# A decoder layer in split float32: the low part of half of w_down's weights made by ACT and a GpSimd DMA

## The chip, the cores and the metric

One core of a Trainium2 chip runs the kernel. The metric is the device time of one execution in microseconds (us); lower is better.

## The reference

One layer of a hybrid decoder on 256 tokens of 2048 features, in float32. Two token mixers run side by side, their gated sum goes through `w_out`, and then come an MLP and a gated embedding:

```python
h = rmsnorm(x, g_mix);  proj = h @ w_in
ya = dilated_mixture(qa, ka, va);  yb = stick_breaking(qb, kb, vb)
x = x + (sigmoid(ga) * (ya @ w_branch_a) + sigmoid(gb) * (yb @ w_branch_b)) @ w_out
x = x + square(relu(rmsnorm(x, g_mlp) @ w_up)) @ w_down
x = x + (p @ w_ple_proj) * sigmoid(rmsnorm(x, g_ple) @ w_ple_gate)
```

`w_up` is 2048 x 8192 and `w_down` 8192 x 2048.

## The kernel before

Every product is made from float32r parts. A number is written as a high part (its rounding to float32r) and a low part (the number minus the high part), both float32r. A product of weight and activation is the sum of three products of parts: high with high, high with low, low with high. In `group_t` the high part of a weight tile of 128 x 128 meets both parts of the activation at once, 512 columns (line 135), and the low part of the weight meets the high part of the activation, 256 columns (line 136). These two matmuls are called a pair here. A group gives two output tiles of 128 features and goes over 16 k tiles, so it has 32 pairs.

Weights come in loads of 1 MB (8 k tiles of 256 columns) into a tile `raw`, by DMAs that SP issues (line 88). `split_weights` cuts a load into two halves of 1024 columns each. For each half, ACT copies `raw` into `wh`, which rounds it (line 79), and VectorE (DVE) writes `wl = raw - wh` (line 80). The tags `raw`, `wh` and `wl` have three buffers each, in the pool `wts`; a buffer is used again when its last reader is done: PE for `wh` and `wl`, ACT and DVE for `raw`.

The MLP goes by quarters of its 8192 hidden features. A quarter is 8 groups of `w_up` (its result, squared and split, is `u`), then 8 groups of `w_down`, each over the quarter's 16 k tiles: two loads a group, `c` = 0 and 1. `residual` adds a group's result to `x` (ACT copies one half out of PSUM, line 447, and DVE adds twice, lines 448 and 449). In the last quarter it also splits the next product's input `h3` (lines 82 and 83) and adds up squares on GpSimd (Pool): `xq` and `acc` (lines 457 and 458).

Large activations lie in blocks of 8 KB per partition, of which the pool `blk` has 15: `x` takes 2, `h`, `m`, `h2`, `u` and `h3` 4 each, `ya`, `yb` and the gate `ga` 2 each, and `qT`, `kT`, `va`, `qS`, `kS`, `vb` one each. Small tiles of 256 columns share the tag `w1` with 8 buffers.

The order of the instructions on each engine is made by the tile framework's planner from the program's order, the buffers that are free and its own costs; each engine then runs its queue in order and waits on semaphores. `later` and `advance` put the attention heads and the embedding's products between the groups by estimated times.

Of the kernel before, what the change touches and what calls it, by code (L numbers as in the profile page):

```python
# [10 lines left out]
F32R = mybir.dt.float32r  # L11
# [5 lines left out]
P = 128  # L17
# [42 lines left out]
def layer_kernel(ctx: ExitStack, tc: tile.TileContext, xt, pt, gains, qkg, cst,  # L60
                 wa, wb, wba, wbb, wo, wup, wdn, wpg, wpp, out):
    nc = tc.nc
    const = ctx.enter_context(tc.tile_pool(name="const", bufs=1))
    blk = ctx.enter_context(tc.tile_pool(name="blk", bufs=15))
    wts = ctx.enter_context(tc.tile_pool(name="wts", bufs=3))
# [10 lines left out]
    def split(hi, lo, src, scale=None):  # L76
        """src (times a per-partition scale) as the exact sum of two float32r parts."""
        if scale is None:
            nc.scalar.activation(hi, src, AF.Copy)  # L79
            nc.vector.tensor_tensor(lo, src, hi.bitcast(F32), op=ALU.subtract)  # L80
        else:
            nc.scalar.activation(hi, src, AF.Copy, scale=scale)
            nc.vector.scalar_tensor_tensor(lo, src, scale, hi.bitcast(F32),  # L83
                                           op0=ALU.mult, op1=ALU.subtract)
# [5 lines left out]

    def split_weights(raw, nk, cols, step=None):
        """The two parts of each k tile of a loaded weight."""
        step = step or 1024 // cols
        parts = []
        for k0 in range(0, nk, step):
            n = min(step, nk - k0)
            wh = wts.tile([P, n, cols], F32R, tag="wh", name="wh")
            wl = wts.tile([P, n, cols], F32R, tag="wl", name="wl")
            split(wh, wl, raw[:, k0:k0 + n, :])
            parts += [(wh[:, i, :], wl[:, i, :]) for i in range(n)]  # L100
        return parts

    def weights(src, nk, cols):
        return split_weights(load(src, nk, cols), nk, cols)

# [3 lines left out]
    def later(us, fn, *args):  # L109
        """Emit fn once the products emitted from here on take this long on the tensor engine."""  # L110
        pending.append((clock[0] + us, len(pending), fn, args))
# [14 lines left out]
    def group_t(chunks, rhs, tag="mm"):  # L126
        """Two feature-major output tiles [P, 512]: columns 0:256 and 256:512 add up to the result.
        A chunk is a source in memory or the parts of its k tiles."""
        ps = [bank(tag) for _ in range(2)]
        last, kt = len(rhs) - 1, 0  # L130
        for src in chunks:
            for wh, wl in src if isinstance(src, list) else weights(src, 8, 256):
                for j in range(2):
                    c = slice(j * P, (j + 1) * P)
                    nc.tensor.matmul(ps[j], wh[:, c], flat(rhs[kt]), start=kt == 0, stop=False)  # L135
                    nc.tensor.matmul(ps[j][:, :T], wl[:, c], rhs[kt][:, 0, :], start=False,  # L136
                                     stop=kt == last)
                kt += 1
                advance(0.65)
        return ps  # L140

    def group_m(chunks, lhs, load=lambda src: weights(src, 4, 512)):
        """Token-major output [2][P tokens, 512 columns]."""
        ps = [bank("mm") for _ in range(2)]
        last, kt = len(lhs) - 1, 0
        for src in chunks:
            for wh, wl in load(src):
                for tt in range(2):
                    t = slice(tt * P, (tt + 1) * P)
                    nc.tensor.matmul(ps[tt], lhs[kt][:, 0, t], wh, start=kt == 0, stop=False)  # L150
                    nc.tensor.matmul(ps[tt], lhs[kt][:, 0, t], wl, start=False, stop=False)  # L151
                    nc.tensor.matmul(ps[tt], lhs[kt][:, 1, t], wh, start=False, stop=kt == last)  # L152
                kt += 1
                advance(1.3)
        return ps

    def halves(ps):
        """Sum of the two halves of a feature-major result, in SBUF."""
        t = work.tile([P, T], F32, tag="w1", name="ev", bufs=W1)
        s = work.tile([P, T], F32, tag="w1", name="es", bufs=W1)  # L160
        nc.scalar.activation(t, ps[:, T:], AF.Copy)  # L161
        nc.vector.tensor_tensor(s, ps[:, :T], t, op=ALU.add)  # L162
        return s

    def rsqrt(y, v, n):
        """y = v ** -0.5, [P, n]; v is kept."""
        s = work.tile([P, n], F32, tag=f"rs{n}", name="rs_s", bufs=1)
        nc.scalar.activation(s, v, AF.Sqrt)
        nc.vector.reciprocal(y, s)
        nc.vector.tensor_tensor(s, y, y, op=ALU.mult)  # L170
        nc.vector.tensor_tensor(s, s, v, op=ALU.mult)
        nc.vector.tensor_scalar(s, s, -0.5, 1.5, op0=ALU.mult, op1=ALU.add)
        nc.vector.tensor_tensor(y, y, s, op=ALU.mult)

    def norm_rows(sq, tag):
        """Reciprocal root mean square of each token, on all partitions: [P, T]."""
        ps = bank("at")
        nc.tensor.matmul(ps[:, :T], ones, sq, start=True, stop=True)
        v = work.tile([P, T], F32, tag="w1", name="nv", bufs=W1)
        nc.vector.tensor_scalar(v, ps[:, :T], 1.0 / D, EPS, op0=ALU.mult, op1=ALU.add)  # L180
        rb = work.tile([P, T], F32, tag="rb", name=tag, bufs=1)
        rsqrt(rb, v, T)
        return rb

# [1 line left out]
    x = [block([P, 8, T], F32, f"x{i}") for i in range(2)]  # L186
# [21 lines left out]

# [1 line left out]
    h = new_acts("h")  # L210
# [4 lines left out]
    def first_weights(c):  # L215
        """x and the first weights in turn, in the order in which the products take them."""
        k = 4 * c
        if c == 0:
            raw = wts.tile([P, 4, 512], F32, tag="raw", name="raw")
            for a, b in ((0, 1), (1, 2), (2, 4)):  # L220
                load_x(a, b)
                nc.sync.dma_start(raw[:, a:b, :].rearrange("p k c -> p (k c)"),
                                  wa[0, 0, :, a * 512:b * 512])
        else:
            load_x(k, k + 4)
            raw = load(wa[0, c], 4, 512)
        for i in range(k, k + 4):
            split(h[i][:, 0, :], h[i][:, 1, :], xs(i), gn[:, 0, i:i + 1])
        if c == 3:
            nc.sync.dma_start(cs, cst)  # L230
            nc.sync.dma_start(gq, bass.AP(tensor=qkg.tensor, offset=qkg.offset,
                                          ap=[[0, P], [DH, 2], [1, DH]]))
        return split_weights(raw, 4, 512, 1 if c == 0 else 2)
# [22 lines left out]

# [1 line left out]
    qT = block([P, NH, T], F32, "qT")  # L258
# [56 lines left out]
    def attend(y, hd, at, v):  # L315
        """y[hd] = (at^T @ v)^T, at [keys, 0:256] for the first key tile, [keys, 256:384] for the second."""
        o = bank("at")
# [70 lines left out]

# [1 line left out]
    ya = new_acts("ya", NH)  # L390
# [11 lines left out]

# [1 line left out]
    yb = new_acts("yb", NH)  # L404
# [21 lines left out]

# [1 line left out]
    m = new_acts("m")  # L428
# [15 lines left out]
    def residual(k, ps, h, gain, acc):  # L444
        """x += result; the next product's input, and the sum of squares."""
        t = work.tile([P, T], F32, tag="w1", name="ev", bufs=W1)
# [21 lines left out]

# [1 line left out]
    em, eparts = [], []  # L470
# [23 lines left out]

# [1 line left out]
    for q in range(4):  # L496
# [14 lines left out]
        for g in range(8):  # L511
            ps = group_t([wdn[g, 2 * q + c] for c in range(2)], u)
            for j in range(2):
                residual(2 * g + j, ps[j], h3 if q == 3 else None, 2, acc)
    later(8, lambda: rbs.append(norm_rows(acc, "rb2")))

# [1 line left out]
    def gate_out(k, s):  # L518
        """out = x + embedding * sigmoid(gate / rms), the gate from memory or accumulators."""
        g = work.tile([P, T], F32, tag="w1", name="g", bufs=W1)  # L520
# [22 lines left out]
def tiles_t(w, nk=8):  # L543
    """[K, N] -> [N / 256, K / (128 nk), 128, nk 256]: what one load takes is contiguous."""
    k, n = w.shape
# [4 lines left out]
def tiles_m(w):  # L550
    """[K, N] -> [N / 512, K / 512, 128, 4 512]."""
    k, n = w.shape
# [4 lines left out]
def columns(a):  # L557
    """[T, K] -> [128, K / 128, T]."""
    t, k = a.shape
# [40 lines left out]
```

## Time and profile before

| what | value |
|---|---|
| median of 3 runs | 1495.04 us |
| lowest and highest run | 1492.69 and 1505.25 us |
| span of the profiled execution | 1494.2 us |
| PE, DVE, ACT, Pool busy in it | 1480.9, 1007.3, 783.1, 133.7 us |
| DMA queue of SP | 275.76 MB, 52.3% of 16 engines |

The profile is one execution. Its span is the time from its first to its last instruction, and it has no other time of its own. PE is the matmul engine, PEld its weight loads, which overlap with matmuls. A busy PE is not PE at its peak, because matmuls are pipelined and their ends are modelled.

### The profile page before, as it was taken

What the parts mean: (1) busy time and instruction counts of PE and PEld (TensorE: products, weight loads), DVE (VectorE), ACT (ScalarE), POOL (GpSimd) and SP (SyncE); (2) the same over time, 40 slices, a digit from 0 to 9 for tenths busy, and PEclk for the clock granted to TensorE, in tenths of its full rate; (3) what the DMA queues carried; (4) which work ended last, traced back from release to release, by engine and by line L of the source; (5) the groups of instructions that cost most, each with busy time, mean ns of one, the idle gap of its engine ahead of it and who ended that gap; (6) DMA issues with size and microseconds to landing.
All of it is one profiled execution on the core that took longest, in us unless ns stands there. A gap on an engine that the chain in (4) does not pass through costs nothing.

```text
span 1494.2 us, 20920 instructions
## 1 busy us (share of the span) xinstructions
PE 1480.9 (99%) x8252; PEld 1285.3 (86%) x8252; DVE 1007.3 (67%) x1463; ACT 783.1 (52%) x1130; POOL 133.7 (9%) x137
## 2 busy tenths in 40 slices
PE   8999999999999999999999999999999999999998
PEld 6788888888888888888888888888888888888887
DVE  7875666466676667767766567656676567777776
ACT  6454554489845555555544445444454445555553
POOL 3432000000000000441000000000000000024200
PEclk9999999999999999999999999999999999999999
DMA  7455444544455555555555555555555555555563
GB/s 297 150 193 190 173 157 163 191 170 168 153 193 197 174 193 188 179 197 175 193 197 187 184 194 197 184 185 196 194 182 189 197 179 187 198 177 189 189 211 109
DMA packets 41281, 277.10 MB, mean 185 GB/s; under 512 B 4704, under 2 KB 7136, under 8 KB 8288
## 3 DMA queue, kind: packets, MB, share of 16 engines
q1 hardware_dynamic: 41040, 275.76, 52.3%
q8 instruction: 64, 1.05, 0.3%
q14 instruction: 33, 0.27, 0.1%
q10 hardware_dynamic: 144, 0.02, 0.0%
HBM read 273.67 MB, written 2.10 MB: 185 GB/s over the span
## 4 chain that ended last, share of the span: by engine, by line
PE 96%; DVE 2%; DMA 0%; ACT 0%; POOL 0%; issue 0%; SPq 0%; ACTq 0%; DVEq 0%; POOLq 0%
PE ps_mm L135 55%; PE ps_mm L136 28%; PE ps_mm L151 3%; PE ps_mm L152 3%; PE ps_mm L150 3%; DVE wl L80 1%; PE ps_at L135 0%; DMA x<-in_xt 0%; PE ps_at L319 0%; DVE h L83 0%; PE ps_mm L537 0%; PE ps_mm L539 0%; PE ps_mm L538 0%; PE ps_at L136 0%; PE ps_at L320 0%
## 5 line engine op out<-in xcount | busy, mean ns | idle before, releaser
L80 DVE TENSOR_TENSOR wl<-raw,wh 128x1024 fp32r<-128x1024 f32 (+1 forms) x518 | 636.2, 1229 | 361.6 <-ACT wh L79 355.2
L79 ACT ACTIVATE wh<-raw 128x1024 fp32r<-128x1024 f32 (+1 forms) x518 | 546.1, 1055 | 461.4 <-PE ps_mm L135 369.8
L135 PE MATMUL ps_mm<-h,wh 128*128 128x512 f32 x2016 | 712.3, 397 | 0.0
L136 PE MATMUL ps_mm<-h,wl 128*128 128x256 f32 x2016 | 564.7, 280 | 0.0
L135 PEld LDWEIGHTS ps_mm<-h,wh 128*128 128x128 f32 x2016 | 377.8, 187 | 87.0 <-ACT wh L79 0.3
L136 PEld LDWEIGHTS ps_mm<-h,wl 128*128 128x128 f32 x2016 | 380.8, 189 | 0.5
L135 PE MATMUL ps_mm<-u,wh 128*128 128x512 f32 x1024 | 356.9, 393 | 0.0
L136 PE MATMUL ps_mm<-u,wl 128*128 128x256 f32 x1024 | 286.9, 280 | 0.0
L135 PEld LDWEIGHTS ps_mm<-u,wh 128*128 128x128 f32 x1024 | 191.7, 187 | 43.6
L136 PEld LDWEIGHTS ps_mm<-u,wl 128*128 128x128 f32 x1024 | 193.5, 189 | 0.0
L161 ACT ACTIVATE ev<-ps_mm 128x256 f32<-128x256 f32 x158 | 59.7, 378 | 91.9 <-PE ps_mm L136 91.9
L150 PE MATMUL ps_mm<-wh,h 128*128 128x512 f32 x256 | 101.7, 400 | 2.6 <-ACT wh L79 2.6
L151 PE MATMUL ps_mm<-wl,h 128*128 128x512 f32 x256 | 101.5, 397 | 2.0 <-DVE wl L80 1.9
L454 POOL TENSOR_TENSOR acc<-x 128x256 f32<-128x256 f32 x2 | 3.3, 1653 | 1112.9 <-DVE x L449 1112.9
L152 PE MATMUL ps_mm<-wh,h 128*128 128x512 f32 x256 | 101.4, 396 | 0.0
L162 DVE TENSOR_TENSOR es<-ps_mm,ev 128x256 f32<-128x256 f32 x158 | 66.4, 421 | 44.2 <-ACT ev L161 44.0
L135 PE MATMUL ps_mm<-m,wh 128*128 128x512 f32 x256 | 90.5, 399 | 0.0
L136 PE MATMUL ps_mm<-m,wl 128*128 128x256 f32 x256 | 71.9, 281 | 0.0
L150 PEld LDWEIGHTS ps_mm<-wh,h 128*128 128x128 f32 x256 | 49.0, 192 | 14.8 <-ACT wh L79 4.9
L447 ACT ACTIVATE ev<-ps_mm 128x256 f32<-128x256 f32 x80 | 30.3, 379 | 59.0 <-PE ps_mm L136 59.0
L151 PEld LDWEIGHTS ps_mm<-wl,h 128*128 128x128 f32 x256 | 49.0, 191 | 13.8 <-DVE wl L80 3.8
L135 PEld LDWEIGHTS ps_mm<-m,wh 128*128 128x128 f32 x256 | 48.1, 188 | 12.1
(159 smaller groups left out, 1181.9 us busy)
## 6 DMA issues: line engine op xcount, KB each, us to landing
raw<-in_wup SPq DMA_DIRECT2D x64, 1024.0 KB, 4.7
raw<-in_wdn SPq DMA_DIRECT2D x64, 1024.0 KB, 4.8
raw<-in_wb SPq DMA_DIRECT2D x48, 1024.0 KB, 4.8
raw<-in_wa SPq DMA_DIRECT2D x31, 1024.0 KB, 4.8
raw<-in_wo SPq DMA_DIRECT2D x16, 1024.0 KB, 4.7
raw<-in_wpg SPq DMA_DIRECT2D x16, 1024.0 KB, 4.8
raw<-in_wba SPq DMA_DIRECT2D x8, 1024.0 KB, 4.7
raw<-in_wbb SPq DMA_DIRECT2D x8, 1024.0 KB, 4.7
```

What stands on the lines that cost most here:

```text
L79: nc.scalar.activation(hi, src, AF.Copy)
L80: nc.vector.tensor_tensor(lo, src, hi.bitcast(F32), op=ALU.subtract)
L135: nc.tensor.matmul(ps[j], wh[:, c], flat(rhs[kt]), start=kt == 0, stop=False)
L136: nc.tensor.matmul(ps[j][:, :T], wl[:, c], rhs[kt][:, 0, :], start=False, stop=kt == last)
L150: nc.tensor.matmul(ps[tt], lhs[kt][:, 0, t], wh, start=kt == 0, stop=False)
L151: nc.tensor.matmul(ps[tt], lhs[kt][:, 0, t], wl, start=False, stop=False)
L152: nc.tensor.matmul(ps[tt], lhs[kt][:, 1, t], wh, start=False, stop=kt == last)
L161: nc.scalar.activation(t, ps[:, T:], AF.Copy)
L162: nc.vector.tensor_tensor(s, ps[:, :T], t, op=ALU.add)
L447: nc.scalar.activation(t, ps[:, T:], AF.Copy)
L454: nc.gpsimd.tensor_tensor(acc, xs(k), xs(k), op=ALU.mult)
```

## The change

In `w_down`, the load `c` = 0 of each group gets its low part in another way. ACT writes the negated, rounded weight into `wl` (a copy with scale -1), then `wh` as before, and a DMA issued from GpSimd adds `raw` to `wl` in place. DVE's subtraction falls away there. The load `c` = 1 is split as before, and so are all other weights. The tags `wh` and `wl` get a fourth buffer, in the whole kernel, and the pool of blocks goes from 15 to 14. A source given to `group_t` may now be a function, called when its turn comes.

```diff
-    blk = ctx.enter_context(tc.tile_pool(name="blk", bufs=15))
+    blk = ctx.enter_context(tc.tile_pool(name="blk", bufs=14))
...
-    def split_weights(raw, nk, cols, step=None):
+    def split_weights(raw, nk, cols, step=None, by_dma=False):
...
-            wh = wts.tile([P, n, cols], F32R, tag="wh", name="wh")
-            wl = wts.tile([P, n, cols], F32R, tag="wl", name="wl")
-            split(wh, wl, raw[:, k0:k0 + n, :])
+            wh = wts.tile([P, n, cols], F32R, tag="wh", name="wh", bufs=4)
+            wl = wts.tile([P, n, cols], F32R, tag="wl", name="wl", bufs=4)
+            if by_dma:
+                src = raw[:, k0:k0 + n, :]
+                nc.scalar.activation(wl, src, AF.Copy, scale=-1.0)
+                nc.scalar.activation(wh, src, AF.Copy)
+                nc.gpsimd.dma_start(wl.rearrange("p k c -> p (k c)"),
+                                    src.rearrange("p k c -> p (k c)"), accum_op=ALU.add)
+            else:
+                split(wh, wl, raw[:, k0:k0 + n, :])
...
-    def weights(src, nk, cols):
-        return split_weights(load(src, nk, cols), nk, cols)
+    def weights(src, nk, cols, by_dma=False):
+        return split_weights(load(src, nk, cols), nk, cols, by_dma=by_dma)
...
-            for wh, wl in src if isinstance(src, list) else weights(src, 8, 256):
+            parts = src if isinstance(src, list) else src() if callable(src) else weights(src, 8, 256)
+            for wh, wl in parts:
...
-            ps = group_t([wdn[g, 2 * q + c] for c in range(2)], u)
+            ps = group_t([lambda c=c: weights(wdn[g, 2 * q + c], 8, 256, by_dma=c == 0)
+                          for c in range(2)], u)
```

## Rows read from the trace of the kernel before

**Rows 1.** The page's busy table and the head of its chain.
```profile
PE 1480.9 (99%) x8252; PEld 1285.3 (86%) x8252; DVE 1007.3 (67%) x1463; ACT 783.1 (52%) x1130; POOL 133.7 (9%) x137
...
PE 96%; DVE 2%; DMA 0%; ACT 0%; POOL 0%; issue 0%; SPq 0%; ACTq 0%; DVEq 0%; POOLq 0%
```

**Rows 2.** Timeline of PE in two w_down stages: start us, us, engine, line, op, tiles.
```profile
784.74 0.39 PE L135 MATMUL ps_mm<-u,wh 128*128 128x512 f32 x1
...
814.90 0.39 PE L135 MATMUL ps_mm<-u,wh 128*128 128x512 f32 x1
...
1375.72 0.40 PE L135 MATMUL ps_mm<-u,wh 128*128 128x512 f32 x1
...
1383.84 0.40 PE L135 MATMUL ps_mm<-u,wh 128*128 128x512 f32 x1
```

**Rows 3.** Stretches: us; busy PE, PEld, DVE, ACT, POOL; granted clock; DMA share; GB/s.
```profile
20.00:30.00 10.00, 8.54 (x36) 6.39 (x36) 10.00 (x11) 6.10 (x11) 5.74 (x6) 1.00 0.67 247
10.00:20.00 10.00, 8.38 (x34) 6.11 (x33) 8.35 (x11) 9.85 (x19) 6.66 (x8) 1.00 1.01 422
763.50:852.00 88.50, 88.50 (x513) 78.05 (x512) 53.41 (x68) 39.12 (x50) 0.00 (x0) 1.00 0.54 191
1310.00:1399.00 89.00, 89.00 (x506) 77.13 (x505) 63.63 (x81) 44.95 (x63) 33.36 (x27) 1.00 0.53 188
```

**Rows 4.** Waits between 662 and 1400 us: total us, times, longest.
```profile
ACT wh L79 <- PE ps_mm L135: 257.4, 189, 1.8
DVE wl L80 <- ACT wh L79: 192.7, 158, 1.8
...
PEld ps_mm L135 <- ACT wh L79: 0.3, 1, 0.3
```

**Rows 5.** Groups of instructions in 763.5 to 852 us: busy us, mean ns.
```profile
L80 DVE TENSOR_TENSOR wl<-raw,wh 128x1024 fp32r<-128x1024 f32 x32 | 39.2, 1225 | 29.6 <-ACT wh L79 29.2
L79 ACT ACTIVATE wh<-raw 128x1024 fp32r<-128x1024 f32 x32 | 33.9, 1060 | 37.2 <-PE ps_mm L135 37.2
...
L447 ACT ACTIVATE ev<-ps_mm 128x256 f32<-128x256 f32 x14 | 5.3, 381 | 10.3 <-PE ps_mm L136 10.3
```

**Rows 6.** Timeline of ACT in the first w_down.
```profile
799.73 1.06 ACT L79 ACTIVATE wh<-raw 128x1024 fp32r<-128x1024 f32 x1 [1.40 <-PE ps_mm L135]
```

**Rows 7.** The tile `raw`: issues by SP, ns min/median/max, first and last start.
```profile
L88 SPq DMA_DIRECT2D raw<-in_wdn x64: 327/328/328, 746.9 to 1376.4; - x64
```

**Rows 8.** Timeline of a group's end in the last w_down, without PE.
```profile
1342.70 0.38 ACT L447 ACTIVATE ev<-ps_mm 128x256 f32<-128x256 f32 x1 [1.46 <-PE ps_mm L136]
...
1344.14 1.62 POOL L457 TENSOR_TENSOR xq<-x 128x256 f32<-128x256 f32 x1 [5.95 <-ACT wh L79]
...
1345.84 0.81 POOL L458 TENSOR_TENSOR acc<-acc,xq 128x256 f32<-128x256 f32 x1
...
1347.01 1.61 POOL L457 TENSOR_TENSOR xq<-x 128x256 f32<-128x256 f32 x1 [0.36 <-DVE x L449]
...
1354.01 0.38 ACT L447 ACTIVATE ev<-ps_mm 128x256 f32<-128x256 f32 x1 [1.47 <-PE ps_mm L136]
```

**Rows 9.** DMA issues: count, KB each, median us from issue to landing.
```profile
raw<-in_wdn SPq DMA_DIRECT2D x64, 1024.0 KB, 4.8
...
x<-in_xt SPq DMA_DIRECT2D x3, 512.0 KB, 10.0
...
raw<-in_wa SPq DMA_DIRECT2D x1, 512.0 KB, 6.4
```

**Rows 10.** DMA in 786 to 842 us, 40 slices of 1.4 us.
```profile
GB/s 117 410 222 0 135 427 187 0 152 410 187 0 199 398 164 0 176 415 164 0 228 410 111 0 205 427 117 12 246 398 105 18 222 427 88 47 234 421 47 41
```

**Rows 11.** Waits of SP's DMA queue between 662 and 1400 us.
```profile
SPq L88 <- DVE wl L80: 523.0, 102, 6.3
```

**Rows 12.** Waits of PE's weight loads in the whole span.
```profile
PEld ps_mm L150 <- ACT wh L79: 4.9, 3, 3.1
...
PEld ps_mm L151 <- DVE wl L80: 3.8, 5, 1.8
```

## The prediction

> **What bounds the kernel now.** I read the busy table first, then the chain that ended last, then the waits, and only then the stretch that is changed. The busy table puts the tensor engine (PE) at 1480.9 of 1494.2 us and VectorE (DVE) at 67%; the chain is 96% PE and 2% DVE [rows 1]. So 13.3 us is all the time in which PE does nothing. Busy PE rows can hide stalls, since a matmul's end is modelled, so the pace was counted from starts: in w_down 87 pairs of products (one with `wh`, one with `wl`) lie between 784.74 and 814.90 us, 0.3467 us a pair; near the end of the last w_down 23 pairs take 8.12 us, 0.353 each [rows 2]. The granted clock is 1.00, the 2.4 GHz level, in both stretches [rows 3], so these two paces are not two clock levels. At either pace no pair waits for weights. The table of waits for 662 to 1400 us says the same: ACT waits 257.4 us for PE to give a `wh` buffer back, DVE waits 192.7 us for ACT, and the only wait of PE's side for weights is one of 0.3 us [rows 4]. The weights are made ahead of need, and DVE has time over.
>
> What this means for the change: DVE's work in w_down is not on the path that sets the end. Freeing it can win nothing there by itself. The question is only whether the new way to a low part is still early enough.
>
> **What is removed.** A load is 8 k tiles and makes two pairs of tiles of 4 k tiles each, which I call splits; a group is four splits, s0 to s3, and there are 4 x 8 = 32 groups of w_down. In s0 and s1 DVE's subtraction goes: 64 times 1.225 us, 78 us in all [rows 5]. It lies beside PE's work and is worth 0 us of the end. It would be worth more only if PE waited for `wl` in w_down.
>
> **What is added on ACT.** 64 copies of 1.06 us [rows 5]. ACT is busy 39.12 of 88.5 us in the first w_down [rows 3]; per group of 11.1 us that is four copies and two evictions, 4 x 1.06 + 2 x 0.38 = 5.0 us, and becomes 7.1 us. In the last w_down ACT has 44.95 us in 89 [rows 3], and 8 x 2.12 = 17 us are added: 62 of 89. ACT has room, so 0 us by itself. An eviction `ev` queued behind the two copies starts at most 2.1 us later; PE takes a bank again only a group later, since there are four banks for two a group, so this too is covered.
>
> **The new chain to a low part.** A `wl` buffer is given back when PE has ended its split. With 4 buffers in place of 3 the buffer is needed again three splits later: 3 x 8 pairs x 0.3467 = 8.32 us. In that time must go:
> - The negated copy: the ACT copies start on PE's release now [rows 6]; with 0.1 us for that, an estimate, and 1.06 us for the copy it is 1.16. Ahead of it on ACT stands at best nothing, at worst the other copy of 1.06 us; I take one eviction, 0.4 [rows 5].
> - The issue on Pool. No row of before shows a DMA issued from there. SP's issue takes 0.33 us and a short Pool operation on 256 columns 0.81, a long one 1.62 [rows 7, 8]. Between 0.33 and 1.62 I take 1.0, an estimate nearest to the short Pool operation, since a queue's issue is not vector work but runs on that engine.
> - The addition's landing. No row shows one. A 1 MB load lands 4.8 us after its issue [rows 9]; the engines move 422 GB/s when full [rows 3], so 2.5 us of the 4.8 are transfer and 2.3 are fixed. An addition of 512 KB moves half the bytes of a load: 2.3 + 1.25 = 3.5 us is the lower end. But it reads two operands, `raw` and `wl`, so it reads as much as a 1 MB load: 4.8 us alone. It isn't alone: the engines are 0.54 occupied [rows 3], in bursts of 400 GB/s with gaps between [rows 10]. The upper end is the 512 KB of x that landed in 10.0 us with others in the engines all the time; a 512 KB load beside less of that took 6.4 us [rows 9]. I take 6.4, nearest to 4.8 plus half of a neighbour's 2.5 us.
>
> Low end 1.16 + 0.33 + 3.5 = 5.0; taken 1.16 + 0.4 + 1.0 + 6.4 = 8.96; upper end 1.16 + 1.06 + 1.62 + 10.0 = 13.8 us, against 8.32. The period of a group is the larger of its PE time and 2.77 us (the split itself) plus the chain. s0 and s1 have this loop each, side by side, so the excess counts once a group: 0 at the low end, 0.64 us taken, 5.5 us at the upper. Times 32 groups: 0, **20.5** and 176 us.
>
> The Trainium skill, DMA: Bandwidth & Descriptors, section "Anatomy of one DMA — SWDGE (gpsimd) path", gives about 2.0 us fixed plus bytes at 436 GB/s for a DMA from this queue, which for 512 KB is an estimate of 3.2 us; no run here shows it yet, and with it the chain would end 3 us early and cost nothing. The same page says under "Issuing engines are not separate DMA queues" that such transfers share the 16 engines with the loads, which speaks against the change where a load is in flight.
>
> **Where loads go.** SP now waits 523.0 us for DVE's `wl` between 662 and 1400 us [rows 11], because that frees a `raw` buffer. For s0 and s1 it will wait for the addition. Queued behind SP's waiting instruction are only the next loads. With landing at 6.4 the buffer of an added load comes free about 1.5 us into the next group, and that of the other load at 2.3 us (s3's copy and subtraction behind the group's start). Both loads of a group then run at once, from about 3 to 8 us, which is when the additions of s0 (issue near 4) and s1 (near 7) run. This is why I take a shared landing and not 4.8. The loads keep their slack: with three `raw` buffers each is issued most of a group before its first copy. Cost beyond the above 0; if the cover is gone, it shows as ACT waiting for `raw`.
>
> **Pool in the last w_down.** There `xq` and `acc` of each group's two tiles take 1.62 + 0.81 + 1.61 + 0.81 = 4.85 us of 11.31, from 1344.14 on, 1.4 to 6.8 us after the first eviction at 1342.70 [rows 8]. The additions for the next group become ready near 4 and 7 us, within this. What stands behind a waiting issue on Pool is `xq` and `acc`, needed only for the norm after the stage. If an issue stands behind one tile's pair it waits up to 2.4 us, if ahead 0; I take 0.8 for 7 groups, **5.6** us (0 to 17).
>
> **The fourth buffer and the 15th block.** Elsewhere in the kernel a fourth buffer could shorten waits for weights: in the whole kernel PE's side waits 4.9 us for `wh` and 3.8 for `wl` [rows 12], near the start, where DVE is busy 10.00 of 10 us [rows 3]; another buffer gives DVE no time. 0, with a gain of at most 7 us. With 14 blocks, the second tile of `ga` has no place until `qS` and `kS` are free: x 2, h 4, ya 2, qS, kS, vb, yb 2 and ga 2 make 15. Its first writer comes with the fifth gate group and the last reader of `qS` with the eighth; meanwhile six `es` tiles must wait, in a tag of 8. So it fits, with two left: 0, and one group of 13 us if it doesn't.
>
> **Sum.** 20.5 + 5.6 = 26 us on the profiled 1494.2, which lies 0.8 below the median 1495.0: **1520 us**, its own range 1506 to 1560.
>
> **The rivals.** *Hidden.* If the addition lands like a lone load, the chain is 1.16 + 0.4 + 1.0 + 4.8 = 7.4 us, below 8.32, and PE never waits: 1495, with the pace of PE and the fourth buffer 1486 to 1505. It decides at a landing of 5.8 us. For it: in most cycles the engines stand still for a slice of 1.4 us or nearly [rows 10]. Against it: the shifted loads fill them at the wrong time. The Trainium skill, Collectives: The Full Stack, "Why ReduceScatter is half of AllGather", holds that an addition in the DMA costs two reads and no more; by this it would come out hidden wherever no load is beside it.
>
> *Additions far slower than loads.* If they land in 8 us or more, or Pool spends over 2 us on each, each further us costs 32 us: 1560 at 7.7 us, 1670 at the upper end. For it: nothing in this trace shows the rate of an addition, and all of it is between tiles on the chip. Against it: no row.
>
> *PE's pace.* Two paces stand in the trace, 0.3467 and 0.353 us a pair [rows 2], and I don't know what turns one into the other; stalls may. All of w_up and w_down from 763 to 1310 us at the slower one would cost 1.8% of 547, 10 us; the last w_down at the faster one would give back 1.6 [rows 3]. With the 7 of the fourth buffer the best that I can build is 1486, so over 1% faster needs something that no row shows.
>
> **How the numbers follow.** Forecast 0.42, hidden 0.36, far slower 0.19, faster by what no row shows 0.03. One per cent, 15 us, is about what this measurement can tell from no change: three runs lie between 1492.69 and 1505.25. Within 1% (to 1510) are the hidden case and a seventh of the forecast: 0.42; slower 0.55. The range 1488 to 1580 leaves out the far upper ends and the few below.
>
> **What would show it.** Right: in w_down PE waits of 0.3 to 1.5 us before the `wl` product or its weight load, put down to the DMA that writes `wl`, once a group, group period 11.4 to 12.5 us in place of 11.1; landing of the additions 5.5 to 7.5 us; DVE near 36% in w_down (53.41 - 16 x 1.225 = 33.8 us of some 94); w_up unchanged at 0.3467. More waits in the last w_down than in the first would show Pool's order. Hidden: no such wait, landing below 5.8. Wrong outright: the loss in w_up or the attention stage, or a wait of ACT for `raw` or of DVE for `ga`.

## The result, and the profile after

The changed kernel takes 1574.8 us (median; 1569.73 to 1578.86), the kernel before 1495.4 beside it: a ratio of 1.051, 95% interval 1.0461 to 1.0558. The forecast was 1520. Slower was right and the range holds it, but the loss is 79 us where 25 were forecast. The profiled execution took 1578.86 us, its span 1577.1.

The page of the changed kernel: span, busy table, two of its DMA queues, the head of its chain, the group of the new issue on Pool, and two kinds of DMA issue (count, KB, median us from issue to landing).

```profile
span 1577.1 us, 21213 instructions
...
PE 1511.3 (96%) x8252; PEld 1300.5 (82%) x8252; DVE 929.2 (59%) x1399; ACT 843.1 (53%) x1194; POOL 179.6 (11%) x201
...
q1 hardware_dynamic: 41040, 275.76, 49.6%
q0 software_dynamic: 9216, 33.56, 10.8%
...
PE 76%; DMA 13%; issue 7%; DVE 2%; ACT 1%; POOL 1%; SPq 0%; POOLq 0%; ACTq 0%; DVEq 0%
...
L104 POOL DMA_DIRECT2D wl<-raw x64 | 55.2, 863 | 680.4 <-ACT wl L102 475.1
...
raw<-in_wdn SPq DMA_DIRECT2D x64, 1024.0 KB, 5.6
...
wl<-raw POOLq DMA_DIRECT2D x64, 512.0 KB, 8.2
```

Against [rows 1] DVE has lost its 78 us, as forecast, and that bought nothing. The chain, 96% PE before, is 13% DMA now. An addition lands 8.2 us after its issue starts; all additions together take 10.8% of the 16 engines' span, 0.108 x 1577.1 / 64 = 2.66 us of full engines for each. The 82.9 us by which the span has grown are of two kinds: PE is idle 65.8 us in place of 13.3, 52.5 more, and busy 30.4 us longer with the same 8252 products.

Stretches of the changed kernel, columns as in [rows 3]: all that lies ahead of the first w_down, the first w_down, the w_up behind it.

```profile
0.00:763.00 763.00, 754.19 (x4054) 646.29 (x4055) 520.37 (x774) 436.32 (x645) 95.14 (x108) 1.00 0.53 186
...
763.00:873.00 110.00, 98.17 (x517) 83.55 (x516) 36.84 (x55) 52.29 (x64) 11.99 (x14) 0.94 0.81 228
873.00:964.00 91.00, 91.00 (x516) 78.75 (x514) 59.22 (x91) 46.51 (x66) 1.72 (x2) 1.00 0.56 190
```

The loss is in w_down alone; there the DMA engines are 0.81 occupied, 0.54 before [rows 3], and the granted clock has a mean of 0.94. From the start of each group's first eviction the groups can be timed: seven periods take 77.65 us in the first w_down of before, 98.25, 95.82, 100.36 and 97.33 in the four of after. A group takes 14.0 us on average in place of 11.15; over the 28 periods that is 79.7 of the 82.9 us.

The waits between 700 and 1480 us, then those of SP's queue from 755 to 862 us, around the first w_down.

```profile
PE ps_mm L145 <- DMA wl<-raw: 50.1, 21, 3.1
...
PEld ps_mm L145 <- issue: 35.8, 12, 3.4
...
PEld ps_mm L145 <- DMA wl<-raw: 10.9, 4, 3.1
...
ACT wh L79 <- DMA raw<-in_wdn: 1.0, 1, 1.0
```
```profile
SPq L88 <- DMA wl<-raw: 87.6, 7, 13.3
SPq L88 <- DVE wl L80: 5.4, 1, 5.4
```

PE waits for the added low part, up to 3.1 us at a time. And SP, which waited for DVE [rows 11], waits for the additions, once a group. What that does is seen in one group. These are rows of the timelines of PE, SP, ACT and Pool, put in order of time: two waits of PE, two releases of SP, and the copies and additions between.

```profile
804.59 0.36 PE L145 MATMUL ps_mm<-u,wl 128*128 128x256 f32 x1 [2.19 <-DMA wl<-raw]
...
807.05 0.80 SPq L88 DMA_DIRECT2D raw<-in_wdn  x2
...
808.56 1.06 ACT L103 ACTIVATE wh<-raw 128x1024 fp32r<-128x1024 f32 x1 [5.12 <-issue]
...
809.52 1.04 ACT L102 ACTIVATE wl<-raw 128x1024 fp32r<-128x1024 f32 x1
...
810.86 0.85 POOL L104 DMA_DIRECT2D wl<-raw  x1 [11.22 <-ACT wl L102]
...
814.01 0.86 POOL L104 DMA_DIRECT2D wl<-raw  x1 [2.29 <-ACT wl L102]
...
818.52 0.35 PE L145 MATMUL ps_mm<-u,wl 128*128 128x256 f32 x1 [1.02 <-DMA wl<-raw]
...
820.97 0.80 SPq L88 DMA_DIRECT2D raw<-in_wdn  x2
```

And the DMA view of 800 to 840 us, one slice a microsecond.

```profile
DMA  9999981079999999995002799999999996027999
GB/s 258 225 213 217 213 176 25 0 164 426 426 442 426 307 213 213 209 213 107 12 4 41 205 385 451 336 262 238 246 217 205 229 205 119 8 66 197 418 434 418
```

SP issues both loads of a group together, at 807.05 and again at 820.97, 13.92 us later. The second row shows what lies between. Some 1.6 us after the issue the loads flow, at 426 GB/s and for 4.9 us (2.1 MB). The additions, issued at 810.86 and 814.01, follow at 213 GB/s: 1.05 MB, 4.9 us, until about 818.5. Then the engines stand still for some 2.4 us until the second addition has landed, SP sees it and issues the next two loads. 1.6 + 4.9 + 4.9 + 2.4 = 13.8. The next group shows the same tie in another shape. The issues on Pool and by SP, and the only DMA queue with packets from 825.5 to 827.8 us:

```profile
823.62 0.86 POOL L104 DMA_DIRECT2D wl<-raw  x1 [8.75 <-ACT wl L102]
...
826.45 0.86 POOL L104 DMA_DIRECT2D wl<-raw  x1 [1.97 <-ACT wl L102]
...
834.88 0.80 SPq L88 DMA_DIRECT2D raw<-in_wdn  x2
```
```profile
q1 hardware_dynamic: 73, 0.60, 102.0%
```

Its additions are issued sooner, but the packets are still the loads' alone, now at some 260 GB/s, and the next release comes 13.91 us after the last. Before, the loads came one by one with gaps [rows 10] and nothing followed on them.

Most of the longer PE time is the clock's. Two stretches behind the stall that ended at 804.59, and the starts of products in them and behind the stall that ended at 818.52:

```profile
806.00:809.00 3.00, 3.00 (x11) 2.52 (x11) 0.00 (x0) 0.44 (x1) 0.00 (x0) 0.50 0.31 63
809.20:818.00 8.80, 8.30 (x48) 6.97 (x47) 1.81 (x3) 5.47 (x7) 1.71 (x2) 1.00 1.04 317
```
```profile
806.56 0.63 PE L144 MATMUL ps_mm<-u,wh 128*128 128x512 f32 x1
...
809.48 0.40 PE L144 MATMUL ps_mm<-u,wh 128*128 128x512 f32 x1
...
817.11 0.40 PE L144 MATMUL ps_mm<-u,wh 128*128 128x512 f32 x1
...
818.71 0.40 PE L144 MATMUL ps_mm<-u,wh 128*128 128x512 f32 x1
...
829.31 0.40 PE L144 MATMUL ps_mm<-u,wh 128*128 128x512 f32 x1
```

From 806 to 809 us the granted clock is 0.50, the 1.2 GHz level, and a pair takes 0.64 us in place of 0.35. The mean granted clock of the whole run is 0.985, before it was 0.998. So some 41 us more stand at the lower level, and products run some 19 us longer there; both are estimates from these means and the two speeds of a pair. The other 11 us or so are lost at 1.00, and part of them is pace: 22 pairs from 809.48 to 817.11 us take 0.347 us each, and 30 from 818.71 to 829.31 take 0.353. These are the two paces of [rows 2], and what turns one into the other stays open.

### The profile page after: what moved, and what is told of

Read it like the earlier page. It is cut to its first block, busy times and chain, and to the rows that moved or that the text cites. A ratio compares the mean times of both kernels' runs of the same rounds, so it can differ in the third digit from the quotient of the medians.

```text
span 1577.1 us, 21213 instructions
## 1 busy us (share of the span) xinstructions
PE 1511.3 (96%) x8252; PEld 1300.5 (82%) x8252; DVE 929.2 (59%) x1399; ACT 843.1 (53%) x1194; POOL 179.6 (11%) x201
## 3 DMA queue, kind: packets, MB, share of 16 engines
q0 software_dynamic: 9216, 33.56, 10.8%
q8 instruction: 65, 1.06, 0.3%
## 4 chain that ended last, share of the span: by engine, by line
PE 76%; DMA 13%; issue 7%; DVE 2%; ACT 1%; POOL 1%; SPq 0%; POOLq 0%; ACTq 0%; DVEq 0%
PE ps_mm L144 42%; PE ps_mm L145 21%; DMA wl<-raw 13%; PE ps_mm L160 3%; PE ps_mm L161 3%; PE ps_mm L159 3%; DVE wl L80 1%; DVE h L83 1%; PE ps_at L144 0%; DMA x<-in_xt 0%; PE ps_at L328 0%; ACT wh L79 0%; ACT wl L102 0%; PE ps_mm L549 0%; PE ps_mm L548 0%
## 5 line engine op out<-in xcount | busy, mean ns | idle before, releaser
L80 DVE TENSOR_TENSOR wl<-raw,wh 128x1024 fp32r<-128x1024 f32 (+1 forms) x454 | 560.2, 1235 | 487.1 <-ACT wh L79 480.2
L79 ACT ACTIVATE wh<-raw 128x1024 fp32r<-128x1024 f32 (+1 forms) x454 | 478.2, 1054 | 355.0 <-PE ps_mm L144 209.7
L144 PE MATMUL ps_mm<-u,wh 128*128 128x512 f32 x1024 | 379.6, 412 | 0.0
L145 PE MATMUL ps_mm<-u,wl 128*128 128x256 f32 x1024 | 298.0, 291 | 52.4 <-DMA wl<-raw 50.1
L145 PEld LDWEIGHTS ps_mm<-u,wl 128*128 128x128 f32 x1024 | 202.7, 198 | 60.2 <-issue 35.8
L144 PEld LDWEIGHTS ps_mm<-u,wh 128*128 128x128 f32 x1024 | 202.0, 197 | 48.9
L103 ACT ACTIVATE wh<-raw 128x1024 fp32r<-128x1024 f32 x64 | 67.9, 1061 | 125.6 <-issue 64.3
L104 POOL DMA_DIRECT2D wl<-raw x64 | 55.2, 863 | 680.4 <-ACT wl L102 475.1
L102 ACT ACTIVATE wl<-raw 128x1024 fp32r<-128x1024 f32 x64 | 66.7, 1043 | 0.0
```

The lines of the kernel that those rows point to most:

```text
L102: nc.scalar.activation(wl, src, AF.Copy, scale=-1.0)
L103: nc.scalar.activation(wh, src, AF.Copy)
L104: nc.gpsimd.dma_start(wl.rearrange("p k c -> p (k c)"), src.rearrange("p k c -> p (k c)"), accum_op=ALU.add)
```

## The experiments

Two explanations stood against each other. **The order**: the landing of a group's second addition releases the loads, these run ahead of the next additions, and the four transfers stand in series, which closes into a cycle. **The engines' time**: before, a group took 0.54 x 11.09 = 6.0 us of the engines; two additions of 2.66 make it 11.3, more than PE's 11.09. Beside them the steps of the prediction: the copies' order on ACT, the fourth buffer, Pool. Each ratio is to runs of the kernel before on the same chip. "A group" is the mean of 28 periods, 7 in each w_down, timed as above; where the last w_down stands by itself, the first figure is of the other three. "Landing" is the page's median for the 512 KB DMAs into a low part, from the start of the issue (in e9 those of the first three w_down).

| kernel | ratio (95%) | a group, us | landing, us |
|---|---|---|---|
| before | 1 | 11.15 | - |
| changed | 1.051 (1.0461 to 1.0558) | 13.99 | 8.2 |
| e1_buffers_only | 0.9956 (0.9922 to 0.9989) | 11.15 | - |
| e2_negated_first | 1.0485 (1.0431 to 1.0539) | 13.95 | 9.0 |
| e3_deep | 1.0374 (1.0327 to 1.042) | 11.6; last w_down 16.5 | 6.4 |
| e4_plain_copy | 1.0004 (0.9979 to 1.0029) | 11.35 | 3.8 |
| e6_no_loads | 1.0011 (0.9981 to 1.0041) | 11.12 | 4.6 |
| e7_first_half | 1.0011 (0.9984 to 1.0039) | 11.18 | 5.1 |
| e8_raw_apart | 1.0672 (1.0625 to 1.0719) | 12.3; last 17.4 | 5.3 |
| e9_raw_apart_deep | 1.0441 (1.039 to 1.0493) | 11.0; last 17.6 | 8.0 |
| e10_four_raw | 1.0484 (1.0439 to 1.0529) | 13.68 | 7.8 |
| e11_one_load | 0.9994 (0.9966 to 1.0023) | 11.26 | 4.6 |
| e12_raw_apart_deep_3q | 1.0092 (1.0063 to 1.012) | 10.8; last 11.3 | 8.3 |
| e5_both_loads | 1652.3 us, one run | 16.2 | 9.1 |
| e13_three_quarters | 1.0128 (1.0104 to 1.0152) | 12.22 | 6.2 |
| e14_unread_second | 1.0087 (1.0072 to 1.0102) | 11.55 | 6.1 |

**e1_buffers_only.** The fourth buffers and 14 blocks, all low parts by DVE: `by_dma=False`.

> Edit: the changed kernel with DVE's subtraction in all loads again; the fourth buffer of wh and wl and the 14 blocks stay. Theory loop (the time is lost in the round of one wl buffer: s0's products on PE, two copies on ACT, the issue, the landing of the addition, 13.4 to 13.9 us in place of 11.1): this kernel has no such round, 1488 to 1498 us. Rival buffers (part of the loss is the 15th block or the new order of the queues): 1505 or more.

Faster by 0.4%, 1493.45 us against 1504.72. The loss is all in the additions. The 0.4% is small beside the spread of runs of one kernel (1490.52 to 1506.5 us here, 1494.09 to 1506.51 before), and a group takes 11.15 us as before, so no gain of the buffers is shown in w_down.

**e2_negated_first.** ACT makes the negated copy ahead of the high part.

```
neg = nc.scalar.activation(wl, src, AF.Copy, scale=-1.0)
with tc.issue_after(neg.ins):
    nc.scalar.activation(wh, src, AF.Copy)
```

> Edit: on ACT the negated copy stands ahead of the copy to wh (in the changed kernel the planner put it behind). Theory loop: the round is shorter by one copy, 0.96 us; times 32 groups 31 us, and up to 48 if the stalls that are left also pull the clock down less: 1527 to 1545 us. Rival engines full (loads and additions together use up the DMA engines, share 0.80 to 0.83 in w_down): the order of two copies changes nothing, 1568 to 1580.

No gain, and the first theory, the round of one `wl` buffer, fails with it: the round is a copy shorter and a group still takes 13.95 us. Issued a copy earlier, the addition lands that much later, the mark of a queue. Below, its addition, and PE's wait for it; SP had issued two loads at 808.20 and 808.62.

```profile
809.91 0.85 POOL L108 DMA_DIRECT2D wl<-raw  x1 [10.12 <-ACT wl L105]
...
820.45 0.38 PE L149 MATMUL ps_mm<-u,wl 128*128 128x256 f32 x1 [3.43 <-DMA wl<-raw]
```

**e4_plain_copy.** The addition becomes a copy: `accum_op=ALU.add` goes.

> Edit: the DMA from GpSimd copies raw over wl and does not add, so the low part is left out (it is the weight itself). Bytes read by it halve. Theory loop with an addition that costs two reads (2.4 us of the engines for 512 KB in the changed kernel's trace): the landing falls from 8.2 to 6 to 7 us, the round to 11.4 to 12.3: 1505 to 1540 us. Rival issue (the software queue's own delay is what makes the landing long): landing stays above 7.7 and the time above 1560.

The loss is gone. Its queue and its SP waits in the first w_down:

```profile
q0 software_dynamic: 9216, 33.56, 6.1%
```
```profile
SPq L88 <- DMA wl<-raw: 76.3, 8, 11.3
```

The same bytes take 1.43 us of engines each, near half of an addition's 2.66. SP still waits for them once a group, so this wait by itself does no harm: the series has to be long as well.

**e6_no_loads and e7_first_half.** In e6 the loads of a quarter's first group serve all eight groups (`kept.append(load(...))`, taken again by each); e7 adds only the first half of each added load (`if by_dma and k0 == 0:`).

> Edit: in w_down the two loads of a quarter's first group serve all eight groups, so the additions run with no loads beside them (the products of w_down use wrong weights). Shows an addition's landing by itself. Theory raw ring: landing about 5.9 us (0.86 issue, 2.5 data, 2.3 to landing), the wl round 2.8 + 2.3 + 5.9 = 11.0 us, hidden: 1488 to 1502 us. Rival wl round with a landing that is 8 us by itself: landing above 7.5 and 1540 or more.

> Edit: only the first half of the load is made by ACT and the GpSimd DMA, the second half by ACT and DVE as before. Theory raw ring: one addition less in the chain, 1.7 + 5.0 + 2.45 + 2.3 = 11.45 us a group: 1498 to 1515 us. Rival wl round: the first half's buffer goes the same round as in the changed kernel, so most of the loss stays, 1545 or more. Rival engines full (0.8 of the share with two additions): falls with the bytes to 1495.

Both without a loss. An addition with no load beside it lands in 4.6 us, 0.86 of it the issue on Pool. One addition a group, beside both loads, lands in 5.1. So neither the addition nor its chain is slow; in these kernels it takes two additions and two loads a group to make the loss. The first w_down of e7 has the engines at 0.77, so one addition adds 0.23 x 11.09 = 2.55 us to a group:

```profile
786.00:841.00 55.00, 55.00 (x319) 48.10 (x318) 26.42 (x35) 28.39 (x35) 4.28 (x5) 1.00 0.77 239
```

**e3_deep, e8_raw_apart and e9_raw_apart_deep** spend free blocks on depth: for the added low part (e3, with the negated copies first), for the raw weights of the added load (e8), for both (e9, whose last w_down has only the raw weights apart).

```
wld = block([P, nk, cols], F32R, "wld")      # e3, e9
raw = block([P, nk, cols], F32, "rawb")      # e8, e9: the added load's
```

> Edit: the added low parts of a load go into a block of their own (8 KB of the pool of blocks) and not into the wl buffers, and both negated copies stand ahead of the copies to wh, so an addition need not wait for PE's release of three splits before. Theory loop: with about a group more of lead PE does not wait, 1490 to 1510 us, though additions and loads move the same bytes. Rival engines full: the bytes are the same, so at least 1550.

> Edit: the changed kernel, but the load that is added lands in a block of its own from the pool of blocks and not in one of the three raw buffers, so the next loads need not wait for the additions. Theory raw ring (SP waits for the additions of a group before it issues the next two loads, the additions of the next group get the engines only behind these loads, so a group lasts 1.7 us of a load's latency + 5.0 for two loads + 4.9 for two additions + 2.3 to their landing = 13.9 us): the ring is broken, what is left is the round of a wl buffer with a landing of 6 to 8 us, 11.1 to 12.5 us a group: 1495 to 1540 us. Rival engines full: same bytes, 1560 or more. Rival wl round (the theory of the first runs): that round is unchanged, 1560 to 1580.

> Edit: as the kernel with the load in a block of its own, and in the first three quarters the added low parts also go into a block of their own with both negated copies ahead. Theory raw ring: neither ring is left in three quarters of w_down, and loads and additions need 9.9 us of the engines in a group of 11.1: 1492 to 1515 us. Rival engines full: 1560 or more.

In three quarters e9 has no loss per group, though its additions land late (8.0 us) and its engines are full; from 786 to 819 us PE is busy all the time at a DMA share of 1.02:

```profile
786.00:819.00 33.00, 33.00 (x192) 28.88 (x191) 11.85 (x18) 19.54 (x25) 5.15 (x6) 1.00 1.02 287
```

So full engines alone don't cost a group anything when the additions start early enough. It holds for the eight groups of a stage, whose entry is late (the first eviction comes at 780.39 us, 774.54 before); no run shows a longer row of such groups. e3 comes near that, and ACT's negated copies wait for loads instead (first w_down):

```profile
ACT wld L100 <- DMA raw<-in_wdn: 37.8, 7, 7.2
```

e8 gains less: SP takes its queue in order, and the plain load stands behind the one that waits for an addition (its SP wait from 755 to 862 us):

```profile
SPq L91 <- DMA wl<-rawb: 43.7, 4, 14.1
```

As whole kernels all three miss their forecasts, with 1558.7, 1601.6 and 1564.5 us. The last quarter spoils them (groups of 11 and 22 us in turn in e9). There 13 of the 14 blocks are taken by activations; that this is why was argued from the count, and e12 fits it.

**e10_four_raw.** A fourth `raw` buffer, paid for with a block (13).

> The changed kernel with four raw buffers instead of three (paid for with 13 blocks instead of 14, which may cost some us around the values of the second branch, before w_down). If the count of raw buffers alone is the cause (the load of c1 waits for the additions of c0, and c0's next load stands behind it), the loads are released a group earlier and the groups return to 11.1 us: 1495 to 1510. If the cause is that SP's loads are released by the landing of the additions and so run exactly when the next additions are issued, a fourth buffer changes which load waits but not that it runs in front of the additions: groups stay at 13.5 to 14 us, the additions land in 8, and the kernel takes 1565 to 1580.

This is the order's number, 1572.6 us. SP still waits for the additions once a group (first w_down), and the loads still run in front of them. One more buffer does not take the cause away.

```profile
SPq L88 <- DMA wl<-raw: 97.3, 8, 13.2
```

**e11_one_load.** The plain load is kept from the first group; the added one is loaded each time (`if c == 1 and kept: return split_weights(kept[0], 8, 256)`).

> The changed kernel in which c1's raw weights stay those of the first group of the quarter (so seven of eight loads of c1 are left out and the output is not the reference's), while c0 is loaded and added as before. The additions then stand behind one load of 2.5 us instead of two: by the sum that gives 13.9 us for two loads (1.7 of ACT and issue + 5.0 of loads + 4.9 of additions + 2.3 to land) a group takes 11.4 us, just above PE's 11.09, and the kernel 1500 to 1515. If the loss does not come from loads ahead of the additions but from anything tied to the two additions themselves, the groups stay near 13.9 us and the kernel at 1575.

No loss, landing as if alone: the one load is through when the additions are issued. The sum of the series, 11.4 us, was near 11.26, but so is PE's own slower pace (11.31 in the last w_down of before). But less was asked of the engines too, so this run alone does not separate the two explanations, nor do e4, e6 and e7.

**e12_raw_apart_deep_3q.** e9 with the last w_down left to DVE.

> The change in the first three w_down only, with the raw weights and the low part of the added load in blocks of their own; the last w_down is DVE's. If the loss of the deep version was only the scarcity of blocks in the last quarter, 21 additions a quarter cost nothing but the entry of each quarter (up to 6 us each): 1500 to 1520. If the added traffic itself costs PE time, the groups of the first three quarters are above 11.1 us and the kernel is over 1530.

Within the forecast: slower by 0.9%. Groups cost nothing (that seven periods take less than PE's 77.65 us goes with late first evictions), but the first eviction of the first w_down comes at 779.97 us, 774.54 before: at a quarter's start the additions have no lead. The change can be hidden; in none of these kernels does it pay.

**e5_both_loads.** Additions for all four parts of a group (`by_dma=True`).

> Both loads of each group by negated copy and addition, no part by DVE: four additions a group. If the additions stand behind two loads and then run one after the other at 2.45 us each, a group takes 1.7 + 5.0 + 9.8 + 2.3 = 18.8 us, and the kernel 1495 + 32 x 7.7 = 1740. If only the DMA engines' own work set the pace (two loads 5.0, four additions 9.8), a group takes 14.8 us and the kernel 1615. If additions and loads ran side by side, about 12.5 us a group and 1540.

Slower than the second of the three has it, and yet of its kind: 16.2 us a group against 6.0 + 4 x 2.66 = 16.6 with the measured price of an addition, and the engines never stand still (760 to 890 us, in the first w_down):

```profile
760.00:890.00 130.00, 98.82 (x514) 81.96 (x514) 18.21 (x39) 67.08 (x81) 25.82 (x30) 0.96 1.00 247
```

Here the engines' time is the bound. In the changed kernel, at 0.81, it is not. The longer series of 18.8 us was wrong for this kernel: SP issues its loads one by one, and they run beside the additions.

**e13_three_quarters and e14_unread_second** were made to separate the two. e13 halves the second addition (DVE subtracts the rest). e14 leaves the second low part to DVE, and adds the same 512 KB into a tile that nobody reads.

```
m = n if k0 == 0 else n // 2                 # e13: what the DMA adds
nc.gpsimd.dma_start(spare, raw[...], accum_op=ALU.add)   # e14, for k0 > 0
```

> The changed kernel in which the second addition of each added load takes only half of its part (256 KB); DVE subtracts the other half. A group then asks the DMA engines for 6.0 + 2.7 + 1.3 = 10.0 us of PE's 11.1 (the share of the stretch would be 0.90), where the changed kernel asks for 11.3. If the loss comes from the engines having no time left, it is almost gone: groups of 11.1 to 11.5 us, landing under 6 us, 1495 to 1515. If it comes from the order alone (loads released by the landing of the additions and run in front of the next ones, 1.7 + 5.0 + 3.7 + 2.3 us), a group takes 12.7 us and the kernel 1540 to 1550.

> The kernel with only the first addition of each load, and beside it a second addition of 512 KB into a spare tile that no product reads (DVE makes the second low part); 13 blocks instead of 14. DMA work per group is that of the changed kernel, 11.3 us of PE's 11.1, and the raw buffer is still held until both additions have landed. If full DMA engines and the released loads delay the first addition, the groups are longer than 12.5 us and the kernel 1535 to 1580, though PE waits for one addition a group only. If the loss came from PE's need of the second addition, the groups stay at 11.1 us and the kernel at 1495 to 1505.

Both land between their two forecasts (1523.9 and 1518.8 us), which answers the question in parts. A stretch of their first w_down, e13 and then e14, and what SP and the spare addition of e14 wait for between 700 and 1420 us:

```profile
786.00:841.00 55.00, 51.54 (x291) 44.53 (x292) 21.57 (x33) 28.51 (x37) 7.73 (x9) 1.00 0.78 236
```
```profile
786.00:841.00 55.00, 53.98 (x307) 46.39 (x306) 26.40 (x35) 26.74 (x34) 7.73 (x9) 1.00 0.98 273
```
```profile
SPq L88 <- DMA wl<-raw: 287.6, 32, 10.5
```
```profile
POOL spare L105 <- DMA raw<-in_wdn: 356.1, 30, 105.1
```

e14 has the whole traffic, at 0.98 of the engines, and loses 0.40 us a group of the changed kernel's 2.84. The spare addition stands outside the series: it is issued when its load has landed (30 times of 32), and of the two SP waits for the useful one alone, 32 times in 32 groups. So full engines without the order make about a seventh of the loss. e13 has a fifth of the engines' time free and loses 1.07 us a group, so order costs without full engines. Taking 1.33 us of addition out of the series took 1.77 us off the group; by the order alone it should have been 12.7 and not 12.2.

So the order holds for most of the loss: a group is the four transfers in series as long as that is longer than PE's time. Taken from 14.0 us, one load of 2.5 (e11), one addition of 2.66 (e7) or the 2 x 1.23 between additions and copies (e4) leave 11.3 to 11.5, and these three take 11.18 to 11.35. PE's own time is 11.09 to 11.31, so they fit the sum but don't test it closely. What stays open is the last half microsecond of e13.

## Why the prediction was wrong in size

**What bounds the kernel: right.** DVE's freed work was worth 0. So were ACT's copies (52.29 us busy of 110 in the first w_down), the block given up (754.19 us of PE in the 763 ahead of w_down, and the first eviction at 774.86 us, 774.54 before) and w_up.

**The decision point of 5.8 us was somewhat high.** The sum adds 1.0 us for the issue to the landing, and the page's landing has the issue in it, so the point is 6.8 in the page's terms. With the low parts in the four shared buffers, the kernels that land in 5.1 us or less lose nothing, those at 6.1 and 6.2 lose 1%, those at 7.8 and more 5% or above: the loss begins between 5.1 and 6.1. ACT's two copies, 2.1 us where 1.06 + 0.4 were taken, would put the point near 6.2. The exception among the kernels is e8, with its raw weights elsewhere: its median of 5.3 goes with a loss.

**The step that failed is the landing, and with it "Cost beyond the above 0" for where loads go.** The landing with the issue was taken as 1.0 + 6.4 = 7.4 us and measured 8.2, where a lone addition takes 4.6 (e6); a group was to lose 0.64 us and loses 2.84. The text saw that both loads would run at once when the additions do, and then priced a landing "nearest to 4.8 plus half of a neighbour's 2.5 us", as though the transfers met at random. But they are tied: the addition's landing releases the loads, and the loads delay the next addition, so the delay feeds itself and a shift doesn't die out. The sign that was named for this cost, ACT waiting for `raw`, showed once, for 1.0 us: the loads themselves still came in time. An additive sum of engine times would have warned: 6.0 us of engines a group [rows 3], and two additions that read as much as a load each, 2 x 2.5, make 11.0 of 11.09; the text had both numbers and never put them together. That would have been a sign only, since full engines by themselves make a seventh of the loss (e14).

**The rest of the gap.** ACT made both copies ahead of an addition, 2.1 us where 1.06 + 0.4 were taken, though e2 shows that this is swallowed by the queue. In the sum's own terms the chain is 0.1 + 2.1 + 8.2 = 10.4 us in place of 8.96, so 2.1 us a group over the 8.32. The clock was not in the sum at all: some 19 of the 82.9 us of the profiled span, an estimate, are products that ran at the lower level behind a stall, in stretches like 806 to 809 us. That the range holds the result is owed to the room it left for slow landings and not to this chain of causes.

**Pool in the last w_down: 5.6 us that did not come.** Its seven periods take 97.33 us, the other three 95.82 to 100.36.

**The rivals.** *Hidden* describes e4, e6, e7 and e11, not the change. *Additions far slower than loads* gave 1560 at 7.7 us and 32 for each further one, without the issue. The 8.2 us with it are 7.2 in these terms, so some 1544: it comes nearer, but its price is too low and its reason wrong, since a lone addition lands in 4.6 us, below a load's 4.8. *PE's pace* hardly moved w_up; in w_down it is part of the 11 us that were lost at 1.00.

The Trainium skill, DMA: Bandwidth & Descriptors, "Issuing engines are not separate DMA queues", says that transfers share the 16 engines whoever issues them; the shares of 0.54, 0.77 and 1.02 for none, one and two additions a group agree. Its fit under "Anatomy of one DMA — SWDGE (gpsimd) path", an estimate of 3.2 us for 512 KB, is near the copy's 3.8 with 0.53 of issue in it, but says nothing of additions: 4.6. The Trainium skill, Collectives: The Full Stack, "Why ReduceScatter is half of AllGather", puts the price of an addition at two reads; 2.66 us of engines against 1.43 for a copy agrees.

## What to carry to other kernels

Before work is moved to a DMA, add up the engines' time of one period, old and new, beside the latency of one transfer. Then follow what the new DMA's landing releases: if that is the next load in an in-order queue, and this runs ahead of the next DMA of the same kind, the latencies stand in series, and the period is their sum where that is longer than the rest. One more buffer on the released side doesn't break this (e10); an earlier start of the dependent transfer does (e9).

## What was not expected of the hardware

- An addition by DMA between tiles moves 213 GB/s, its 512 KB counted once, where loads move 426, and 512 KB of it take 2.66 us of full engines, a copy 1.43. The issue on Pool takes 0.86 us, a copy's 0.53.
- After a stall of PE of 2.19 us the granted clock was 0.50 for 3 us, the 1.2 GHz level, and a pair of products took 0.64 us in place of 0.35. The slow products cost some 19 us, an estimate, beside the 52.5 of the stalls.
